# Low halves of the first weight pieces: from GpSimd beside the norm's products to VectorE behind them

## The chip, the cores and the metric
The kernel runs on one core of a Trainium2 chip. A core has TensorE (matrix products, into PSUM), VectorE, ScalarE and GpSimd (work on tiles of 128 rows), and SyncE, which issues transfers. Each engine runs its own instructions in order; semaphores make one wait for another. The profile calls them PE (PEld for its weight loads), DVE, ACT, POOL and SP. The metric is the device time of one execution in microseconds (us), lower is better.

## The reference
A trunk of two layers on x of 256 rows by 2048 columns, float32. Of each layer:

```python
for l in range(DEPTH):                     # 2
    h = rms_norm(x, norm_pre[l])
    proj = jnp.einsum('bsd,de->bse', h, w_in[l])
    (q, kc, vc, ksl, vsl, kwn, vwn, gl, z_att, u_s5, z_s5, u_pool, z_pool) = split(proj)
    att = nsa_mixer(...) * silu(z_att)     # three attention branches, gated
    ssm = s5_mixer(u_s5, ...) * silu(z_s5) # a diagonal state space layer
    pool = pool_mixer(u_pool, ...) * silu(z_pool)
    out = einsum(concatenate([att, ssm, pool]), w_out[l])
    x = x + rms_norm(out, norm_post[l])
```

`rms_norm` divides each row by the root of its mean square and multiplies by a weight per column. Every product with h waits for the norm, and the first norm of layer two waits for the end of layer one.

## The kernel before
Each float32 matrix product is made of three passes: both operands are split into a high part (a rounded copy, "fp32r") and a low part (what is left), and `mm3` (L384 to L389) adds high x high, high x low and low x high. The weights come as a stream of pieces of 2 x 128 x 1024 values per layer, in the order of use: the selected branch's values (`vs`, two pieces, four halves), the S5 input (`u5`, four pieces), keys and values, and so on to the output matrix (`wo`). SyncE loads a half into one of five `raw` buffers (L285); ScalarE makes the high part `whi` (L311); the low part `wlo` is raw minus high, on VectorE (L317) or, where the caller says so, on GpSimd (L315). The low part is the last to read the raw buffer, so it sets when the next load starts. The first three halves of `vs` have their high and low parts in tiles called `m`.

The rows are two tiles of 128. The norm of a tile: ScalarE sums the squares (L930), VectorE and GpSimd make the reciprocal norm (L395, L401, L402 and the power L396), VectorE multiplies x by it and by the weight in four products of 512 columns (`norm_scale`, L408), TensorE transposes the result (L415, through PSUM tiles `tr`, `sc`, `acc`, `sc`), ScalarE makes the high part of the transposed tile hT (L418) and VectorE its low part (L421). Then `vsel` multiplies a quarter of hT with a quarter of the `vs` weights: 12 matrix products (L387 to L389).

The two stages in question are written out by hand, and all five engines keep the written order there (`tc.manual_schedule(engines=ORDERED)`): the start, and the passage from layer one to layer two, where the last output products (`mm_last`), the update of x (L1230) and the next norm are interwoven. Between them a scheduler orders the instructions by its own estimate of the times.

At the start the lows of the four halves of `vs` go to GpSimd:

```python
r = rstd_of(sqs[0], first)
...
for h in range(2):
    split(0, h, True)(G)
...
r = rstd_of(sqs[1])
for h in range(2):
    split(1, h, True)(G)
```

In the passage the first half's low is VectorE's, the other three are GpSimd's. Where the program says `after("pool")`, what follows (S5's memsets L459, L460 and the load L1040) stands behind GpSimd's last instruction of the stage.

Of the kernel before, what the change touches and what calls it, by code (L numbers as in the profile page):

```python
# [17 lines left out]
S, D, NL = 256, 2048, 2  # L18
NKT = D // 128
SCALE = 128 ** -0.5  # L20
EPS = 1e-6
# [7 lines left out]

# column offsets of the input projection  # L30
OQ, OKC, OVC, OKS, OVS, OKW, OVW, OGL, OZA, OU5, OZ5, OUP, OZP = (
# [3 lines left out]
def piece_plan():  # L35
    """Weight pieces of one layer in the order of use: (kind, index, cols per half)."""
    b = [("vs", 0), ("vs", 1)] + [("u5", t) for t in range(4)]
    early = [("kc", 0), ("kc", 1), ("vc", 0), ("vc", 1), ("ks", 0), ("ks", 1), ("kw", 0), ("kw", 1),
             ("vw", 0), ("vw", 1), ("vw", 2)]
    cmp_ = [("ck", i) for i in range(4)] + [("cv", i) for i in range(4)]  # L40
    mid = []
    for i, e in enumerate(early):
        mid.append(e)
        if i >= 2:
            mid += cmp_[:2]
            del cmp_[:2]
    mid += cmp_
    pairs = []
    z5at = (1, 1, 1, 3)
    for p in range(4):  # L50
        pairs += [("q", 2 * p), ("za", 2 * p), ("q", 2 * p + 1), ("za", 2 * p + 1)]
        pairs += [("z5", t) for t in range(4) if z5at[t] == p]
    late = [("z5", t) for t in range(4) if z5at[t] > 3] + [("gl", 0), ("gl", 1)]
    for g in range(4):
        late += [("up", g), ("zp", g)]
    wo = [("wo", c * 4 + i) for c in range(4) for i in range(4)]
    return b + mid + pairs + late + wo
# [18 lines left out]

# columns of the per-layer small parameters
SM = {}
# [5 lines left out]
SMW = _o  # L84
# columns of the per-layer S5 matrices, pool and compression matrices
CBW = 1024
# [51 lines left out]
def body(ctx, tc, a):  # L138
# [39 lines left out]

# [1 line left out]
    cn = const.tile([128, CNW], F32, name="cn")  # L180
# [9 lines left out]

# [1 line left out]
    NP = NL * 16  # L192
# [12 lines left out]
    def after(key):  # L205
        """issue what follows behind the instruction kept under key, on its engine"""
        return tc.issue_after(X[key].ins)

    def s5_params():
# [41 lines left out]
        V.tensor_mul(ci, t2, t0)  # L251
        # cos and sin of 4 theta b and 32 theta a, a and b in 0 .. 7
        pa, pb = (st([128, NP, 16], "P", bufs=2) for _ in range(2))
# [14 lines left out]

# [1 line left out]
    stream = [(l, k, i, PIECE_OFF[n]) for l in range(NL) for n, (k, i) in enumerate(PLAN)]  # L270
# [51 lines left out]

# [1 line left out]
    chains = []  # L324
# [15 lines left out]
    def grab(*tags):  # L340
        """wait until every one of the tags has a free buffer, then hold them"""
        while not all(free(g) for g in tags):
            yield 0.0
        for g in tags:
            take(g)

    def demand(*tags):
        """the same for the stream of pieces: run the chains until the buffers are free"""
        while not all(free(g) for g in tags):
            forced[0] += 1  # L350
            slot(2.0)
        for g in tags:
            take(g)
# [21 lines left out]
    def split_f32r(hi, lo, src, scale=None, hi_eng=None):  # L375
        """hi + lo == src * scale, both float32r"""
        if scale is None:
            A.activation(hi, src, AF.Copy)  # L378
            V.tensor_tensor(lo, src, hi.bitcast(F32), op=ALU.subtract)
        else:  # L380
            A.activation(hi, src, AF.Copy, scale=scale)
            V.scalar_tensor_tensor(lo, src, scale, hi.bitcast(F32), op0=ALU.mult, op1=ALU.subtract)

    def mm3(out, l, r, start, stop, **kw):  # L384
        """three passes: hi*hi, hi*lo, lo*hi"""
        (lh, ll), (rh, rl) = l, r
        T.matmul(out, lhsT=lh, rhs=rh, start=start, stop=False, **kw)  # L387
        T.matmul(out, lhsT=lh, rhs=rl, start=False, stop=False, **kw)  # L388
        T.matmul(out, lhsT=ll, rhs=rh, start=False, stop=stop, **kw)  # L389

# [1 line left out]
    def rstd_of(parts_, first=None):  # L392
        """(sum of the four parts / D + EPS) ** -0.5; first: what rstd_first made of three of them"""
        s = first or rstd_first(parts_)
        V.scalar_tensor_tensor(s[:, 1:2], parts_[:, 3:4], 1.0 / D, s[:, 0:1], op0=ALU.mult, op1=ALU.add)  # L395
        X["pool"] = G.tensor_tensor(s[:, 2:3], s[:, 1:2], mhalf, op=ALU.pow)  # L396
        return s[:, 2:3]
# [7 lines left out]
    def norm_scale(x, r, gpre, hbuf, c):  # L405
        """hbuf = x * r * gpre in quarter c of x and hbuf [128, D]"""
        cs = slice(c * 512, (c + 1) * 512)
        V.scalar_tensor_tensor(hbuf[:, cs], x[:, cs], r, gpre[:, cs], op0=ALU.mult, op1=ALU.mult)  # L408

    def norm_high(t, hbuf, hT, c):  # L410
        """high part of quarter c of hbuf transposed; returns what makes the low part"""
        p = (trp, scp, accp, scp)[c]()
        for j in range(4):
            k = 4 * c + j
            T.transpose(p[:, j * 128:(j + 1) * 128], hbuf[:, k * 128:(k + 1) * 128], ident)  # L415
        sl = (slice(None), slice(4 * c, 4 * c + 4), slice(t * 128, (t + 1) * 128))
        pv = p.rearrange("p (k s) -> p k s", k=4)
        X["act"] = A.activation(hT[0][sl], pv, AF.Copy)  # L418

        def low():  # L420
            X["norm"] = V.tensor_tensor(hT[1][sl], pv, hT[0][sl].bitcast(F32), op=ALU.subtract)  # L421
        return low

    def vsel(n, t, c):
        """values of the selected branch, tile t, from quarter c of hT"""
        if t == 0 and c == 0:
# [4 lines left out]
    def norm_vsel(n, t, x, r, gpre, hbuf, hT, lag):  # L431
        """the norm of tile t and its values, quarter after quarter"""
        low = []
# [13 lines left out]

# [1 line left out]
    def s5_chain(l):  # L449
# [22 lines left out]
        def tables(hf):  # L472
            """cos and sin of 4 theta j, j = 8 a + b, for the state tiles 8 hf .. 8 hf + 7"""
            pa, pb = (z.rearrange("p (i a b) -> p i a b", i=8, a=8) for z in ms[:2])
# [28 lines left out]
        def spread(dst, x, y, op, k0):  # L503
            """x op y, group by group into the block diagonal of dst"""
            V.tensor_tensor(x, x, y, op=op)  # L505
# [42 lines left out]
        for t in range(4):  # L548
# [4 lines left out]
            kb = kbd  # L553
            # transposed input matrices and the lag kernels
            yield from grab("sc")
# [78 lines left out]

# [1 line left out]
    def cmp_blocks(which, g, p, l):  # L636
# [55 lines left out]

# [1 line left out]
    def rope(p, dst_hi, dst_lo):  # L694
# [7 lines left out]

# [1 line left out]
    def att_unit(pr, j, t):  # L704
        """one head of the pair, one tile of queries: scores .. transposed weights"""
        h = 2 * pr["p"] + j
# [4 lines left out]
        p = scp()  # L711
# [129 lines left out]

# [1 line left out]
    def pool_chain(g, l):  # L843
# [35 lines left out]
    def silu2(dst, p):  # L879
        """dst = 2*silu(p)"""  # L880
        A.activation(dst, p, AF.Tanh, scale=0.5)
        V.scalar_tensor_tensor(dst, dst, 1.0, p, op0=ALU.add, op1=ALU.mult)

# [1 line left out]
    def mm_b(n, h, p):  # L885
# [45 lines left out]

    # start
    xt = [a8([128, D]) for _ in range(2)]
# [14 lines left out]
    with tc.manual_schedule(engines=ORDERED):  # L948
# [33 lines left out]
        gp_out(1)  # L982
        for h in range(2):
            split(0, h, True)(G)
        def sq1(c):
# [6 lines left out]
        norm_scale(xt[0], r, gpre, hb[0], 2)  # L992
        norm_scale(xt[0], r, gpre, hb[0], 3)
        sq1(0)
        low = []
# [4 lines left out]
        for f in low:  # L1000
            f()
        r = rstd_of(sqs[1])
        for h in range(2):
            split(1, h, True)(G)
        for c in range(4):
            norm_scale(xt[1], r, gpre, hb[1], c)
        vsel(0, 0, 0)
        vsel(0, 0, 1)
# [15 lines left out]
    while n < nst:  # L1024
# [167 lines left out]
        else:  # L1192
# [32 lines left out]
            def update(t, r, sq=None):  # L1225
                """x += og * r, with the sums of squares or the store"""
                x, og = X["xt"][t], X["og"][t]
# [20 lines left out]
            elif q == 0:  # L1248
# [14 lines left out]
                else:  # L1263
                    m = n + 4
                    sqs = [st([128, 4], "sq", bufs=4) for _ in range(2)]
                    with tc.manual_schedule(engines=ORDERED):
# [12 lines left out]
                        r = rstd_of(sqs[0])  # L1279
                        split(m, 1, True)(G)  # L1280
                        for c_ in range(4):
                            norm_scale(X["xt"][0], r, X["gpre"], X["og"][0], c_)
                        mm_last(1, 2)
                        split(m + 1, 0, True)(G)
                        X["hT"] = hT
                        low = [norm_high(0, X["og"][0], hT, c_) for c_ in range(4)]
                        split(m + 1, 1, True)(G)
                        for f in low:
                            f()
                        mm_last(1, 3)  # L1290
                        first = rstd_first(X["osq"][1])
# [97 lines left out]
```

## Time and profile before

| | |
|---|---|
| time, median of 3 runs | 893.35 us (893.23 to 893.95) |
| span of the profiled execution (the page gives no other time for it) | 890.6 us |
| median less span | 2.75 us |
| TensorE busy | 857.6 us, 96% of the span |
| VectorE busy | 645.3 us, 72% |
| ScalarE busy | 481.3 us, 54% |
| GpSimd busy | 51.8 us, 6% |
| DMA | 165.75 MB, mean 186 GB/s |

A busy share is a mean over stages with different limits. What an engine waits for, and when, stands in the timelines; idle time of an engine that nobody waits for costs nothing.

### The profile page before, as it was taken

How to read it: one execution, taken by the hardware profiler on the slowest of the kernel's cores; microseconds unless marked ns; L12 is line 12 of the kernel's file. 1: busy time of each engine (PE TensorE's matmuls, PEld its weight loads, DVE VectorE, ACT ScalarE, POOL GpSimd, SP SyncE). 2: the span in 40 equal slices, each digit the busy share in tenths (PEclk: the TensorE clock that was granted, in tenths of full speed). 3: DMA queues.
4: the chain of work that ended last, by engine and by line, in shares of the span. 5: the costliest groups of instructions: out<-in, count | busy, mean ns of one | idle time of the engine just before them, and what ended most of it. 6: DMA issues, size and time to landing. Idle time of an engine off the chain costs nothing. (4 is left out here: it accounts for less than half of the span.)

```text
span 890.6 us, 17313 instructions
## 1 busy us (share of the span) xinstructions
PE 857.6 (96%) x6848; PEld 795.3 (89%) x6848; DVE 645.3 (72%) x1264; ACT 481.3 (54%) x933; POOL 51.8 (6%) x71
## 2 busy tenths in 40 slices
PE   4899999999999999999979999999999999999996
PEld 3898889999999999888869988999999999998884
DVE  6886779796987866556478556978968878665563
ACT  5454635676566754445445525475847767344440
POOL 3302000000000000000040300000000000000000
PEclk9899999999999999999989999999999999999998
DMA  7565766524344665456445558663534347455642
GB/s 288 179 188 185 268 235 225 172 104 162 121 165 143 227 241 194 172 201 224 182 165 199 183 197 312 211 213 99 173 123 155 140 144 295 154 177 189 197 146 95
DMA packets 46042, 165.75 MB, mean 186 GB/s; under 512 B 5508, under 2 KB 5764, under 8 KB 44808
## 3 DMA queue, kind: packets, MB, share of 16 engines
q1 hardware_dynamic: 43352, 154.15, 50.3%
q0 software_dynamic: 2608, 10.49, 3.3%
q8 instruction: 54, 0.88, 0.4%
q14 instruction: 28, 0.23, 0.1%
HBM read 159.37 MB, written 4.19 MB: 184 GB/s over the span
## 5 line engine op out<-in xcount | busy, mean ns | idle before, releaser
L311 ACT ACTIVATE whi<-raw 128x1024 fp32r<-128x1024 f32 (+2 forms) x238 | 248.4, 1046 | 256.3 <-PE pp L388 82.8
L317 DVE TENSOR_TENSOR wlo<-raw,whi 128x1024 fp32r<-128x1024 f32 (+1 forms) x236 | 284.4, 1207 | 123.7 <-ACT whi L311 123.1
L389 PE MATMUL pp<-hT,wlo 128*128 128x256 f32 x1280 | 365.7, 286 | 0.5 <-DVE wlo L317 0.5
L387 PE MATMUL pp<-hT,whi 128*128 128x256 f32 x1280 | 364.8, 285 | 0.8 <-ACT whi L311 0.8
L388 PE MATMUL pp<-hT,whi 128*128 128x256 f32 x1280 | 363.5, 284 | 0.0
L387 PEld LDWEIGHTS pp<-hT,whi 128*128 128x128 f32 x1280 | 245.0, 191 | 6.1 <-issue 3.8
L389 PEld LDWEIGHTS pp<-hT,wlo 128*128 128x128 f32 x1280 | 245.0, 191 | 2.4 <-DVE wlo L317 0.7
L388 PEld LDWEIGHTS pp<-hT,whi 128*128 128x128 f32 x1280 | 245.0, 191 | 1.7 <-issue 1.0
L387 PE MATMUL acc<-whi,m 128*128 128x512 f32 x112 | 44.4, 397 | 0.0
L389 PE MATMUL acc<-whi,m 128*128 128x512 f32 x112 | 44.4, 397 | 0.0
L388 PE MATMUL acc<-wlo,m 128*128 128x512 f32 x112 | 44.1, 394 | 0.0
L388 PE MATMUL pp<-wlo,m 128*128 128x512 f32 x112 | 43.6, 389 | 0.0
L389 PE MATMUL pp<-whi,m 128*128 128x512 f32 x112 | 43.6, 389 | 0.0
L387 PE MATMUL pp<-whi,m 128*128 128x512 f32 x112 | 43.6, 389 | 0.0
L507 ACT ACTIVATE m<-m 64x256 f32<-64x256 f32 x64 | 26.4, 413 | 5.9 <-DVE m L505 4.9
L728 ACT ACTIVATE P<-sc,sv 128x128 f32<-128x128 f32 (+1 forms) x64 | 26.2, 418 | 5.4 <-DVE sv L726 3.7
L925 POOL DMA_DIRECT2D a<-in_gpost x2 | 1.1, 557 | 451.4 <-PE tr L743 451.4
L378 ACT ACTIVATE a<-tr 128x256 fp32r<-128x256 f32 (+1 forms) x32 | 15.6, 488 | 18.6 <-PE tr L743 18.5
L387 PEld LDWEIGHTS acc<-whi,m 128*128 128x128 f32 x112 | 21.5, 192 | 4.5
L388 PEld LDWEIGHTS acc<-wlo,m 128*128 128x128 f32 x112 | 21.5, 192 | 4.5
L389 PEld LDWEIGHTS acc<-whi,m 128*128 128x128 f32 x112 | 21.4, 191 | 4.5
L736 ACT ACTIVATE P<-P,sv 128x128 f32<-128x128 f32 (+1 forms) x64 | 25.4, 448 | 0.0
(295 smaller groups left out, 1384.4 us busy)
## 6 DMA issues: line engine op xcount, KB each, us to landing
raw<-in_w SPq DMA_DIRECT2D x272, 512.0 KB, 3.6
raw<-in_w SPq DMA_DIRECT2D x8, 420.0 KB, 4.2
a<-in_x SPq DMA_DIRECT2D x4, 512.0 KB, 6.9
a<-in_gpost POOLq DMA_DIRECT2D x2, 1024.0 KB, 4.8
a<-in_x POOLq DMA_DIRECT2D x2, 1024.0 KB, 6.3
xs<-a SPq DMA_DIRECT2D x2, 1024.0 KB, 4.1
a<-xs POOLq DMA_DIRECT2D x2, 1024.0 KB, 7.4
out_dram<-a SPq DMA_DIRECT2D x8, 256.0 KB, 2.4
```

Source lines behind the costliest of these rows:

```text
L311: A.activation(hi[:, :w], raw[:, :w], AF.Copy)
L317: V.tensor_tensor(lo[:, :w], raw[:, :w], hi[:, :w].bitcast(F32), op=ALU.subtract)
L378: A.activation(hi, src, AF.Copy)
L387: T.matmul(out, lhsT=lh, rhs=rh, start=start, stop=False, **kw)
L388: T.matmul(out, lhsT=lh, rhs=rl, start=False, stop=False, **kw)
L389: T.matmul(out, lhsT=ll, rhs=rh, start=False, stop=stop, **kw)
L507: A.activation(dst[64 * g:64 * g + 64, :, k0:k0 + 4, 16 * g:16 * g + 16], x[64 * g:64 * g + 64], AF.Copy)
L728: A.activation(P[:, b], pv[:, b], AF.Exp, scale=SCALE, bias=sv[:, 1, b:b + 1], accum_out=sv[:, 2, b:b + 1])
L736: A.activation(P[:, b], P[:, b], AF.Copy, scale=sv[:, 4, b:b + 1])
L925: nc.gpsimd.dma_start(g, bass.AP(tensor=src.tensor, offset=src.offset, ap=[[0, 128], [1, D]]))
```

## The change
At the start, the lows of the first `vs` piece are made on VectorE, one behind the products of tile 0 and one behind the hT lows of tile 0; those of the second piece behind the products of tile 1. In the passage, the three lows that were GpSimd's are made on VectorE behind the hT lows of tile 0, and ScalarE's highs for them stand behind its own part of the transposed tile. GpSimd keeps the powers L396, its loads and its memsets. Lines behind the first hunk move by one or two numbers. (Comments were taken out as well; those lines are left out here.)

```diff
         r = rstd_of(sqs[0], first)
         gp_out(1)
-        for h in range(2):
-            split(0, h, True)(G)
+        wlow = [split(0, h, True) for h in range(2)]
+
         def sq1(c):
...
         norm_scale(xt[0], r, gpre, hb[0], 2)
         norm_scale(xt[0], r, gpre, hb[0], 3)
+        wlow[0](V)
         sq1(0)
         low = []
         for c in range(4):
...
         for f in low:
             f()
+        wlow[1](V)
         r = rstd_of(sqs[1])
-        for h in range(2):
-            split(1, h, True)(G)
         for c in range(4):
             norm_scale(xt[1], r, gpre, hb[1], c)
+        for h in range(2):
+            split(1, h)
         vsel(0, 0, 0)
         vsel(0, 0, 1)
...
                         r = rstd_of(sqs[0])
-                        split(m, 1, True)(G)
                         for c_ in range(4):
                             norm_scale(X["xt"][0], r, X["gpre"], X["og"][0], c_)
                         mm_last(1, 2)
-                        split(m + 1, 0, True)(G)
                         X["hT"] = hT
                         low = [norm_high(0, X["og"][0], hT, c_) for c_ in range(4)]
-                        split(m + 1, 1, True)(G)
                         for f in low:
                             f()
+                        split(m, 1)
+                        split(m + 1, 0)
+                        split(m + 1, 1)
                         mm_last(1, 3)
```

VectorE's order at the start before, from the last products of tile 0 (L408 into `a_7_88`) to the first hT low of tile 1 (`hT_85` from `tr_237`):

```order
L408 SCALAR_TENSOR_TENSOR a_7_88<-a_1_82,rs_139,a_11_92 128x512 x2
L421 TENSOR_TENSOR hT_85<-tr_160,hT_84 128x4x128
...
L421 TENSOR_TENSOR hT_85<-sc_182,hT_84 128x4x128
L401 TENSOR_REDUCE rs_194<-sq_87 128x1
...
L408 SCALAR_TENSOR_TENSOR a_8_89<-a_2_83,rs_194,a_11_92 128x512 x4
L421 TENSOR_TENSOR hT_85<-tr_237,hT_84 128x4x128
```

The same place now; `m_26`, `m_27`, `m_37` and `wlo_207` are the lows of the four `vs` halves, `raw_...` their raw buffers:

```order
L408 SCALAR_TENSOR_TENSOR a_7_88<-a_1_82,rs_139,a_11_92 128x512 x2
L317 TENSOR_TENSOR m_26_146<-raw_102,m_26_146 128x1024
L421 TENSOR_TENSOR hT_85<-tr_159,hT_84 128x4x128
...
L421 TENSOR_TENSOR hT_85<-sc_181,hT_84 128x4x128
L317 TENSOR_TENSOR m_27_148<-raw_104,m_27_148 128x1024
L401 TENSOR_REDUCE rs_194<-sq_87 128x1
...
L408 SCALAR_TENSOR_TENSOR a_8_89<-a_2_83,rs_194,a_11_92 128x512 x4
L317 TENSOR_TENSOR m_37_203<-raw_108,m_37_203 128x1024
L317 TENSOR_TENSOR wlo_207<-raw_110,whi_206 128x1024
L421 TENSOR_TENSOR hT_85<-tr_237,hT_84 128x4x128
```

Four L317 have come into this queue; the hT lows are the same as before, with other buffer numbers.

GpSimd's order at the start, before, from the first power to the load of the pool matrices:

```order
L396 TENSOR_TENSOR rs_139<-rs_139,mhalf 128x1
L315 TENSOR_TENSOR m_26_146<-raw_102,m_26_146 128x1024
L315 TENSOR_TENSOR m_27_149<-raw_104,m_27_149 128x1024
L396 TENSOR_TENSOR rs_194<-rs_194,mhalf 128x1
L315 TENSOR_TENSOR m_37_199<-raw_108,m_37_199 128x1024
L315 TENSOR_TENSOR wlo_203<-raw_110,whi_202 128x1024
L1040 DMA pw_430<-in_pw 128x1024
```

Now the four L315 are gone, and the load and the memsets follow the second power directly.

VectorE's order in the passage, from the products of tile 0 of layer two to the last output product of tile 1 (L1222, now L1224):

```order
 L408 SCALAR_TENSOR_TENSOR a_637_4611<-a_643_4619,rs_5213,a_640_4615 128x512 x4
...
+L421 TENSOR_TENSOR hT_5194<-sc_5252,hT_5193 128x4x128
+L317 TENSOR_TENSOR m_759_5262<-raw_5081,m_759_5262 128x1024
+L317 TENSOR_TENSOR m_760_5265<-raw_5087,m_760_5265 128x1024
+L317 TENSOR_TENSOR wlo_5269<-raw_5089,whi_5268 128x1024
 L401 TENSOR_REDUCE rs_5284<-sq_4618 128x1
 L402 TENSOR_SCALAR rs_5284<-rs_5284 128x1
-L1222 TENSOR_TENSOR a_638_4612<-acc_5078,a_639_4613 128x512
+L1224 TENSOR_TENSOR a_638_4612<-acc_5078,a_639_4613 128x512
```

Three L317 now stand between the last hT low of tile 0 and the reciprocal norm of tile 1.

## Rows read from the trace of the kernel before

**Rows 1.** Busy us by stretch: PE, PEld, DVE, ACT, POOL (instructions), granted clock, DMA share, GB/s.

```profile
0.00:40.00 40.00, 24.34 (x140) 22.00 (x141) 29.54 (x53) 19.18 (x37) 15.76 (x17) 0.91 0.68 243
40.00:440.00 400.00, 399.35 (x3256) 371.17 (x3255) 295.55 (x602) 224.13 (x435) 11.46 (x21) 1.00 0.54 189
440.00:475.00 35.00, 28.28 (x168) 25.11 (x167) 26.95 (x41) 18.33 (x36) 13.07 (x12) 0.85 0.44 153
...
25.00:30.00 5.00, 2.96 (x14) 2.99 (x15) 4.84 (x6) 1.87 (x4) 2.98 (x3) 0.57 0.76 261
...
430.00:435.00 5.00, 5.00 (x23) 4.13 (x22) 0.00 (x0) 0.00 (x0) 0.00 (x0) 1.00 0.26 98
...
465.00:470.00 5.00, 4.96 (x28) 4.52 (x29) 3.88 (x7) 1.79 (x3) 0.73 (x2) 0.66 0.45 144
```

**Rows 2.** Timeline of VectorE, first stage: start, us, instruction, count [idle before].

```profile
10.21 3.51 DVE L408 SCALAR_TENSOR_TENSOR a<-a,rs,a 128x512 f32<-128x512 f32 x2
13.65 0.68 DVE L973 COPY a<-pp 128x512 f32<-128x512 f32 x1
...
14.85 2.30 DVE L408 SCALAR_TENSOR_TENSOR a<-a,rs,a 128x512 f32<-128x512 f32 x2
...
20.02 0.14 DVE L401 TENSOR_REDUCE rs<-sq 128x1 f32<-128x3 f32 x1
...
21.29 6.93 DVE L408 SCALAR_TENSOR_TENSOR a<-a,rs,a 128x512 f32<-128x512 f32 x4 [0.67 <-POOL rs L396]
28.14 0.68 DVE L421 TENSOR_TENSOR hT<-tr,hT 128x512 fp32r<-128x512 f32 x1
...
31.57 3.50 DVE L317 TENSOR_TENSOR wlo<-raw,whi 128x1024 fp32r<-128x1024 f32 x3 [0.22 <-ACT whi L311]
```

**Rows 3.** Timeline of GpSimd, first stage.

```profile
10.72 5.21 POOL L315 TENSOR_TENSOR m<-raw,m 128x1024 fp32r<-128x1024 f32 x2 [0.54 <-ACT m L311]
...
23.55 2.80 POOL L315 TENSOR_TENSOR wlo<-raw,whi 128x1024 fp32r<-128x1024 f32 x1
...
27.01 0.97 POOL L459 MEMSET m<- 128x1024 f32 x1
```

**Rows 4.** View of line L408: ns minimum/median/maximum, and who waited for it.

```profile
L408 DVE SCALAR_TENSOR_TENSOR a<-a,rs,a x16: 739/750/2847, 10.2 to 466.9; 128x512 f32<-128x512 f32 x16
...
PE sc L415: 5.9, 3
```

**Rows 5.** Timeline of TensorE, first stage.

```profile
27.04 1.09 PE L415 MATMUL sc<-cn,a 128*128 128x128 f32 x4 [2.13 <-DVE a L408]
...
29.48 0.56 PE L387 MATMUL pp<-m,hT 128*128 128x256 f32 x1
...
32.73 0.28 PE L387 MATMUL pp<-m,hT 128*128 128x256 f32 x1
32.84 0.28 PE L388 MATMUL pp<-m,hT 128*128 128x256 f32 x1
...
39.56 0.28 PE L387 MATMUL pp<-hT,whi 128*128 128x256 f32 x1
```

**Rows 6.** Timeline of VectorE, passage to layer two.

```profile
444.55 6.93 DVE L408 SCALAR_TENSOR_TENSOR a<-a,rs,a 128x512 f32<-128x512 f32 x4 [0.66 <-POOL rs L396]
...
454.36 0.15 DVE L402 TENSOR_SCALAR rs<-rs 128x1 f32<-128x1 f32 x1
457.10 0.69 DVE L1222 TENSOR_TENSOR a<-acc,a 128x512 f32<-128x512 f32 x1 [2.59 <-PE acc L389]
...
464.11 2.08 DVE L408 SCALAR_TENSOR_TENSOR a<-a,rs,a 128x512 f32<-128x512 f32 x3 [0.66 <-POOL rs L396]
```

**Rows 7.** Timeline of TensorE, passage to layer two.

```profile
462.53 0.28 PE L389 MATMUL pp<-whi,hT 128*128 128x256 f32 x1
465.01 0.63 PE L415 MATMUL tr<-cn,a 128*128 128x128 f32 x4 [2.20 <-DVE a L408]
```

**Rows 8.** Busy us of the stretch behind the first norm, columns as in Rows 1.

```profile
31.15:75.63 44.48, 44.48 (x367) 44.48 (x367) 38.70 (x102) 23.21 (x40) 10.71 (x20) 0.98 0.61 190
```

## The prediction
> **What bounds the kernel now.** I read the busy table by stage first [rows 1]. TensorE works 399.35 of the 400 us between 40 and 440, and about as densely in the second layer; it stands still for 15.7 us in the first 40 and for 6.7 us between 440 and 475. So only these two stages, the norms at the head of each layer, can give time back, and all else follows TensorE. The second view was VectorE's timeline in the first stage [rows 2]: its L408 rows are the norm's products (x times reciprocal norm times weight, 512 columns), and they take 3.51 us for two, 2.30 for two and 6.93 for four. The third was GpSimd's timeline beside it [rows 3]: while L315 (a low half) runs, one product gets through, and it ends when L315 ends. The line's own view [rows 4] gives the free price, median 750 ns against a maximum of 2847, and names TensorE's transposes as what waits for them. Then came TensorE around the first stage [rows 5], and VectorE and TensorE around the second [rows 6, 7].
>
> The profiled execution has a span of 890.6 us; the median of the runs is 893.35, so 2.75 lie around the span, and I carry a gain in the span over to the median unchanged.
>
> **The change part by part.** It takes seven L315 off GpSimd (two of them fill 5.21 us) and puts seven L317 of the same shape on VectorE. Three L317 in a row take 3.50, the last of them 1.22 [rows 2], so one costs a queue (3.50 − 1.22) / 2 = 1.14 us. ScalarE's and TensorE's products stay the same in number. No wait on GpSimd is left for a weight low.
>
> *First layer, VectorE's queue.* A free product costs a queue 0.67 (in layer two, with no L315 beside them, three take 2.08 [rows 6], of which the last is 0.74, the line's minimum [rows 4]). From the first product at 10.21 to the first hT low of tile 1 there stand eight products, 8 x 0.67 = 5.36; two copies, 14.85 − 13.65 = 1.20; the four new lows, 4 x 1.14 = 4.56; four hT lows of a copy's shape, 4 x 0.60 = 2.40; and the reciprocal norm, 21.29 − 20.02 = 1.27 [rows 2]. Sum 14.79, so that hT low starts at 25.0, where it stands at 28.14 now: 12.5 of products became 5.36, the lows cost 4.56, and 0.6 of short waits has gone.
>
> *First layer, TensorE.* Its 24 products of the first two weight quarters need the second new low (done near 18.8) and end by 21. The four groups of transposes follow tile 1's products, which now run from 20.0 to 22.8, so they end at 23.5 to 23.9. The third quarter needs the third new low, two places before 25.0: 25.0 − 2 x 1.14 + 1.22 = 23.94. It starts there, and at 29.48 now [rows 5]: 5.5 us. From it to the first product of the next piece stand 72 products, at 0.12 apiece (32.73 to 32.84, rounded) 8.64 us; now they take 39.56 − 29.48 = 10.08, because the first of them ran at half pace after TensorE had waited for the products. The wait for the first hT low (done 25.7, when fourteen products are through) costs about 0.1. So the next piece starts near 32.6 and not 39.56: 7.0 us.
>
> *What is late next there.* TensorE comes 7.0 us earlier to the pieces that follow, VectorE only 31.15 − 27.4 = 3.7 (its four hT lows of tile 1 end the norm). VectorE is busy 38.70 of the 44.48 us that follow, while TensorE never rests [rows 8], so of its 5.8 us of slack it has to win back 3.3 before the S5 tables are used, near 76. Most of that slack is waiting for TensorE to free weight buffers, which now happens earlier. I charge 0.4.
>
> The loads: the first two raw buffers come free near 15.3 and 18.8 instead of at the ends of L315 (near 13.2 and 15.9), so the two pieces that reuse them are issued two to three microseconds later on SP; they are wanted by ScalarE only behind the norm, near 26, and by TensorE after 32. GpSimd's load of the pool matrices and its memset, queued behind L315 until 26.3, come at about 20, beside tile 1's products. The memset of 0.97 us at 27.01 [rows 3] already ran beside two products that took the free 0.67 a step, so I cost it at nothing; held for all of it, one product would add 0.97.
>
> *Second layer.* VectorE's queue from 444.55: four products 2.68, four hT lows 2.40, three new lows 3.42, the two small ones of the reciprocal norm 0.38, so L1222 of tile 1 can start at 453.4, and now starts at 457.10 [rows 6]. TensorE does not hold it: the last product ends at 447.3, its transposes by 448.4, and the twelve output products behind them, at 5.00 / 22 = 0.23 each (23 begin in 5 us [rows 1]), end by 451.2. Three raw buffers are given back by the new lows, two of them some us later than by L315, far ahead of the pieces they are loaded for. ScalarE makes the three highs after the transposed tiles, from 448.7, a microsecond before VectorE comes to the first low, so the lows need not wait. Everything from L1222 to tile 1's transposes is a chain through ScalarE and GpSimd that the change doesn't touch, so it moves by 3.65 us, and the transposes from 465.01 to 461.35.
>
> TensorE, though, finishes its 48 products of tile 0 near 456.9 (451.2 + 48 x 0.12) and then stands some 4.5 us, where it now stands 2.20 [rows 7]. Behind 2.20 us of rest the granted clock reads 0.66 in the next 5 us, that is the lower level of 1.2 GHz for part of it [rows 1]. The Trainium skill ("TensorE: Matmul & The Clock Gate", What's actually happening) says that throttled is the default state and activity releases it, so a longer rest speaks against this part of the change; no run so far shows a rest of 4.5 us here. If the clock behaved as it does now, the stage would win 3.65; if the transposes run at the lower level from the start (1.09 for four at 27.04 against 0.63 at 465.01 [rows 5, 7]), it wins 3.65 less some 0.6. I take the latter, 3.05.
>
> Sum: 7.0 − 0.4 + 3.05 = 9.65 us; the span 881.0, the time 893.35 − 9.65 = 883.7.
>
> **Rivals.**
> *VectorE becomes the bound in layer one.* For it: 38.70 of 44.48 busy [rows 8], and 4.56 us more on its queue. Against: its slack. If it wins nothing back, TensorE keeps VectorE's 3.7 instead of 7.0 and no charge: 3.7 + 3.05, time 886.6.
>
> *TensorE's clock falls in both stages.* For it: the granted clock was 0.57 between 25 and 30 [rows 1], behind a wait of 2.13 [rows 5]. Against: the new waits in stage one are well under a microsecond. If it falls as now, layer one loses the 1.44 of the products (10.08 − 8.64) and three times 0.46 on transposes (1.09 − 0.63 [rows 5, 7]), layer two another 1.2, twice the charge it has: 4.0 back, 887.7.
>
> *The products are slow of themselves (slower).* They might be slowed by the transfers into the same memory, since DMA was busy beside the first four, and not by L315. Then they keep their time, and the lows come on top: 4.56 in layer one; in layer two, 454.36 + 0.2 + 3.42 = 458.0 against 457.10, 0.9. Time 898.8. The point from which it decides: the eight products of layer one cost the queue 12.5 us now (3.44 + 2.21 + 6.85), 1.56 each, so above 1.56 − 4.56 / 8 = 0.99 us apiece the edit loses. Against it: the last four of layer two, without L315 beside them, are at 0.67 [rows 6]. The Trainium skill ("SBUF — State Buffer", Who interferes with whom) describes an exclusive lock between GpSimd's reads and a VectorE operation with two inputs in SBUF, held for a whole instruction; by that the products fall to 0.67 and this rival is void, and the rows, where product and L315 end together, agree.
>
> *Hidden anyway (no change).* If the weight stream set the pace between the norms, an earlier start would be given back in waits for loads. Against: 399.35 of 400 busy, DMA at 0.54 [rows 1]. Time then about 893.
>
> **How the numbers follow.** Forecast 0.60 (its own range 882.0 to 885.5: stage one within a microsecond, the clock of stage two between nothing and 1.3); VectorE's bound 0.20; the clock 0.12; slower 0.04; no change 0.04. The range runs from 881.5 (882.7 with neither charge, and 1.2 for short waits of TensorE that I can't place) to 888.5, which takes in both smaller gains. A measurement tells 0.2%, 1.8 us, from no change: faster 0.92, same 0.04, slower 0.04.
>
> **What would show it.** L408 at 0.75 throughout and no L315; the third quarter's first product near 24 and the next piece near 32.6; no TensorE wait between 33 and 80 longer than half a microsecond; L1222 of tile 1 nine microseconds after the first product of tile 0, directly behind the three lows; a rest of TensorE near 4.5 us before tile 1's transposes. It is wrong if products stay above 1 us, if the TensorE waits move into the S5 part, or if the stage behind the second norm grows by more than the 0.6.

## The result, and the profile after

The kernel after takes 881.58 us (median of 4 runs, 880.47 to 882.04), the kernel before 893.29 beside it: ratio 0.9878, 95% interval 0.9865 to 0.9891. Forecast were 883.7 in a range of 881.5 to 888.5, so the time is 2.1 us below the forecast and at the lower end of the range. The span of the profiled execution went from 890.6 to 880.1 us.

Busy time of the kernel after, first line of its page, then the stretches of [rows 1] (PE, PEld, DVE, ACT, POOL with instructions, granted clock, DMA share, GB/s):

```profile
PE 851.2 (97%) x6848; PEld 790.0 (90%) x6848; DVE 640.5 (73%) x1271; ACT 481.2 (55%) x933; POOL 33.5 (4%) x64
```

```profile
0.00:40.00 40.00, 28.18 (x194) 25.14 (x195) 30.76 (x70) 25.36 (x49) 5.45 (x13) 1.00 0.77 266
40.00:440.00 400.00, 397.73 (x3230) 369.19 (x3229) 296.14 (x599) 221.61 (x432) 12.02 (x22) 1.00 0.57 190
440.00:475.00 35.00, 30.25 (x230) 29.18 (x229) 30.59 (x48) 20.39 (x37) 4.58 (x8) 0.95 0.60 204
25.00:30.00 5.00, 5.00 (x43) 4.99 (x43) 5.00 (x10) 2.79 (x4) 2.00 (x4) 1.00 0.71 213
```

GpSimd fell from 15.76 to 5.45 us in the first 40. VectorE rose by only 1.2 there, though it has four lows of 1.2 more: its eight products of the start fell from 12.7 us (3.51, 2.30, 6.93) to 5.6 (1.42, 1.41, 2.74), and other work came forward into the stretch (70 instructions for 53). TensorE works 28.18 of the first 40 where it worked 24.34 [rows 1], and the stretch from 25 to 30, granted 0.57 before, is full at 1.00. The middle holds a first surprise: TensorE stands still for 2.3 us between 40 and 440 where it stood for 0.65.

The line of the norm's products, which answers to [rows 4], then VectorE in the first stage, which answers to [rows 2]:

```profile
L408 DVE SCALAR_TENSOR_TENSOR a<-a,rs,a x16: 743/746/754, 10.7 to 457.2; 128x512 f32<-128x512 f32 x16
```

```profile
10.66 1.42 DVE L408 SCALAR_TENSOR_TENSOR a<-a,rs,a 128x512 f32<-128x512 f32 x2
...
14.51 1.22 DVE L317 TENSOR_TENSOR m<-raw,m 128x1024 fp32r<-128x1024 f32 x1
...
18.04 1.21 DVE L317 TENSOR_TENSOR m<-raw,m 128x1024 fp32r<-128x1024 f32 x1
...
20.45 2.74 DVE L408 SCALAR_TENSOR_TENSOR a<-a,rs,a 128x512 f32<-128x512 f32 x4 [0.67 <-POOL rs L396]
23.11 1.22 DVE L317 TENSOR_TENSOR m<-raw,m 128x1024 fp32r<-128x1024 f32 x1
24.24 1.22 DVE L317 TENSOR_TENSOR wlo<-raw,whi 128x1024 fp32r<-128x1024 f32 x1
25.38 0.68 DVE L421 TENSOR_TENSOR hT<-tr,hT 128x512 fp32r<-128x512 f32 x1
```

All sixteen products now take 743 to 754 ns; the maximum was 2847. The four of tile 1 take 2.74 us where they took 6.93, the four new lows stand where the order put them, and the first hT low of tile 1 comes at 25.38.

TensorE in the first stage and at the next piece, which answers to [rows 5]:

```profile
19.31 0.39 PE L388 MATMUL pp<-m,hT 128*128 128x256 f32 x1 [0.86 <-DVE m L317]
...
21.35 0.63 PE L415 MATMUL tr<-cn,a 128*128 128x128 f32 x4 [0.46 <-DVE a L408]
...
23.72 0.36 PE L387 MATMUL pp<-m,hT 128*128 128x256 f32 x1
24.38 0.39 PE L388 MATMUL pp<-m,hT 128*128 128x256 f32 x1 [0.29 <-DVE m L317]
...
33.29 0.28 PE L389 MATMUL pp<-hT,wlo 128*128 128x256 f32 x1
```

The third quarter starts at 23.72 (before 29.48), the next piece at 33.29 with two of its products done earlier (before 39.56). Of the waits on VectorE behind tile 0's transposes 0.86, 0.46 and 0.29 are left; the 0.86 is for the second new low, which is done at 18.04 + 1.21 = 19.25.

The passage, VectorE and then TensorE, which answer to [rows 6] and [rows 7]:

```profile
438.27 2.74 DVE L408 SCALAR_TENSOR_TENSOR a<-a,rs,a 128x512 f32<-128x512 f32 x4 [0.66 <-POOL rs L396]
...
443.33 2.36 DVE L317 TENSOR_TENSOR m<-raw,m 128x1024 fp32r<-128x1024 f32 x2
445.61 1.22 DVE L317 TENSOR_TENSOR wlo<-raw,whi 128x1024 fp32r<-128x1024 f32 x1
446.75 0.15 DVE L401 TENSOR_REDUCE rs<-sq 128x1 f32<-128x3 f32 x1
...
447.00 0.68 DVE L1224 TENSOR_TENSOR a<-acc,a 128x512 f32<-128x512 f32 x1
...
453.99 2.08 DVE L408 SCALAR_TENSOR_TENSOR a<-a,rs,a 128x512 f32<-128x512 f32 x3 [0.66 <-POOL rs L396]
```

```profile
454.88 1.08 PE L415 MATMUL tr<-cn,a 128*128 128x128 f32 x4 [4.66 <-DVE a L408]
455.76 1.06 PE L415 MATMUL sc<-cn,a 128*128 128x128 f32 x4
456.62 1.06 PE L415 MATMUL acc<-cn,a 128*128 128x128 f32 x4
457.33 0.56 PE L387 MATMUL pp<-m,hT 128*128 128x256 f32 x1
457.69 0.35 PE L388 MATMUL pp<-m,hT 128*128 128x256 f32 x1
```

L1224 (L1222 before) of tile 1 stands 8.73 us behind the first product of tile 0, where it stood 12.55, directly behind the lows and the small ones. TensorE then rests 4.66 us and comes back at the lower level (1.08 for four transposes); products are short again from 457.69.

To see where the time comes from, I compared the starts of the same ScalarE instructions in two traces. Gain against the kernel before, medians over stretches of before's time:

```
stretch (us)        25-75     150-425   460-500   from 575
after               6.3-6.5   6.28      10.59     10.54
after, second run   6.0-6.2   7.60      11.98     13.13
```

The start gives 6 us by its end and the passage 4.3 to 4.4 in both runs; layer two behind it gives nothing back, and the second run wins 1.2 more there. Between 75 and 150 the two executions of one program differ by 1.3 us, and by 1.2 in layer two: that is how far one profile can be trusted.

### The profile page after: what moved, and what is told of

Its sections match the earlier page's. It is cut to its first block, busy times and chain, and to the rows that moved or that the text cites. A ratio compares the mean times of both kernels' runs of the same rounds, so it can differ in the third digit from the quotient of the medians.

```text
span 880.1 us, 17310 instructions
## 1 busy us (share of the span) xinstructions
PE 851.2 (97%) x6848; PEld 790.0 (90%) x6848; DVE 640.5 (73%) x1271; ACT 481.2 (55%) x933; POOL 33.5 (4%) x64
## 5 line engine op out<-in xcount | busy, mean ns | idle before, releaser
L317 DVE TENSOR_TENSOR wlo<-raw,whi 128x1024 fp32r<-128x1024 f32 (+2 forms) x238 | 286.7, 1207 | 125.7 <-ACT whi L311 125.0
L389 PEld LDWEIGHTS pp<-whi,m 128*128 128x128 f32 x112 | 21.0, 188 | 4.4
```

The costliest lines, as they stand in the source:

```text
L317: V.tensor_tensor(lo[:, :w], raw[:, :w], hi[:, :w].bitcast(F32), op=ALU.subtract)
```

## The experiments

Three comparisons, each with the kernel before beside the others: it measured 891.33, 891.42 and 891.37 us, some 2 us less than beside the first runs of the kernel after, so the ratios to it are what compares. The recorded ratio is not the plain quotient of the two medians; it lies up to 0.0014, or 1.2 us, beside it, and so a gain is good to about a microsecond. The kernel after, run again in the third, measured 880.99 us, 0.9882 (0.9865 to 0.9899).

### The start alone, the passage alone

```diff
 # e1_start: the kernel after, but in the passage as before
                         r = rstd_of(sqs[0])
+                        split(m, 1, True)(G)
...
+                        split(m + 1, 0, True)(G)
...
+                        split(m + 1, 1, True)(G)
-                        split(m, 1)
-                        split(m + 1, 0)
-                        split(m + 1, 1)
 # e2_passage: the kernel before with the opposite edit there
```

> The start of the kernel after, the passage into layer two of the kernel before (its three low halves on GpSimd again). Theory A (the products of the norm take about four times as long while GpSimd makes a low half, at both places and independently): the start's gain alone, read as 6.3 us at L1224 of the first tile, so 893.3 - 6.3 = 887.0 us; the products L408 of the passage stay at 6.93 us for four. Rival B (the two places are worth the same thing only together, since TensorE takes up in one what the other gives): under 884 or over 890.

> The start of the kernel before, the passage of the kernel after. Theory A: the passage's gain alone, read as 4.3 us at the first product of the pair u5 in layer two, so 893.3 - 4.3 = 889.0 us, with the products of the passage at 2.74 us for four and those of the start as before (3.5 and 2.3 us for two). With this and the run of the start alone the two gains should add to the whole of 11.7 us within 1 us. Rival B: they do not add.

Start alone: 882.83 us, ratio 0.9896 (0.9881 to 0.9911), 8.5 us below before. Passage alone: 888.89 us, 0.9965 (0.9951 to 0.9979), 2.4 us. Together 10.9, and the kernel after gained 10.4 in the third comparison: they add within a microsecond, so theory A holds on that. By the ratios they are 9.3 and 3.1, together 12.4 against 10.5, so they add only within two. 882.83 is below the 884 that I had named as rival B's sign; that 884 stood for a gain of 9.3 from 893.3, and the gain here is 8.5 from 891.33, so it does not speak for B. The sizes missed: the start is worth 2.2 more than the 6.3 I had read from one profile, the passage 1.9 less than 4.3. In the start-alone kernel the passage is untouched; VectorE's products there, then TensorE's transposes of tile 1:

```profile
434.96 6.93 DVE L408 SCALAR_TENSOR_TENSOR a<-a,rs,a 128x512 f32<-128x512 f32 x4 [0.67 <-POOL rs L396]
```

```profile
455.08 0.63 PE L415 MATMUL tr<-cn,a 128*128 128x128 f32 x4 [2.21 <-DVE a L408]
455.75 1.09 PE L415 MATMUL sc<-cn,a 128*128 128x128 f32 x4
456.63 1.06 PE L415 MATMUL acc<-cn,a 128*128 128x128 f32 x4
```

The same 6.93 as before, with the start's products at 1.42, 1.41 and 2.74: the slowness belongs to the place where GpSimd's lows are, not to the kernel.

### Is it GpSimd's being busy, its reading, or its two inputs?

```diff
 # e3_memset
-                X["pool"] = G.tensor_tensor(lo[:, :w], raw[:, :w], hi[:, :w].bitcast(F32), op=ALU.subtract)
+                for _ in range(3):
+                    X["pool"] = G.memset(lo[:, :w].bitcast(F32), 0.0)
 # e4_copy
+                X["pool"] = G.tensor_copy(lo[:, :w], raw[:, :w])
```

> The kernel before with each low half of its seven early ones replaced by three fills of the same buffer with zero on GpSimd, at the same place: GpSimd is as busy beside the products but reads nothing. Seven low halves of weights are left out by that. Theory A (what holds VectorE's product is GpSimd's operation with two tensors read, not that GpSimd works): products of the norm at 0.74 us each, no low half in VectorE's queue: 876 to 880 us. Rival E (any work of GpSimd holds a VectorE product): products at 0.97 us or more, 884 us or more.

> The kernel before with GpSimd copying the raw half into the low one (one tensor read) where it subtracted (two tensors read); the seven low halves are then not the ones wanted. Theory A in its narrow form (only two tensors read on GpSimd hold a product with two tensors read on VectorE): products at 0.74 us each, 876 to 880 us. In its wide form (any reading operation of GpSimd holds it): products as long as the copy beside them, 879 to 888 us.

With fills: 876.53 us, 0.9833 (0.9812 to 0.9853). With copies: 883.91 us, 0.9911 (0.9893 to 0.9928). GpSimd and VectorE beside each other, first with the fills (lines are one number higher there):

```profile
19.07 2.97 POOL L316 MEMSET m<- 128x1024 f32 x3
21.98 2.98 POOL L316 MEMSET wlo<- 128x1024 f32 x3
```

```profile
19.15 2.74 DVE L409 SCALAR_TENSOR_TENSOR a<-a,rs,a 128x512 f32<-128x512 f32 x4 [0.67 <-POOL rs L397]
```

and with the copies:

```profile
20.48 1.04 POOL L315 CAST m<-raw 128x1024 fp32r<-128x1024 f32 x1
21.46 1.50 POOL L315 CAST wlo<-raw 128x1024 fp32r<-128x1024 f32 x1
```

```profile
20.57 4.27 DVE L408 SCALAR_TENSOR_TENSOR a<-a,rs,a 128x512 f32<-128x512 f32 x4 [0.67 <-POOL rs L396]
```

Beside 2.97 us of fills the four products take their free 2.74; beside copies that read one tensor, 4.27, two of the four being held to 1.50 and 1.52. So what holds a product is GpSimd reading, with one input as well as with two: the wide form of theory A. Rival E, that any work of GpSimd holds it, is out. The Trainium skill ("SBUF — State Buffer", Who interferes with whom) says the same: a VectorE instruction with two SBUF inputs contends with a GpSimd instruction that reads SBUF, not with one that only writes it. Both runs agree with it. The copy on VectorE at 13.65 in [rows 2], which reads only a PSUM tile, took 0.68 beside a running L315 [rows 3]; that an operation with a single SBUF input goes free as well is not shown here.

The fills leave no low on either engine's way, so the kernel after at 880.99 against 876.53 also says what the seven lows cost on VectorE: 4.5 us of their 8.0 (7 x 1.14). The traces place it in both stages: 2.0 us by 76 us, and 2.6 in the passage, of which some 0.8 is the lower level of TensorE's clock behind the longer rest, which the kernel with fills does not have.

### The lows in front of the products, and the lows twice

```diff
 # e5_front: the kernel before, at all five places
-            split(0, h, True)(G)
+            split(0, h, True)(V)
 # e6_twice: the kernel after, all seven
+                    V.tensor_tensor(lo[:, :w], raw[:, :w], hi[:, :w].bitcast(F32), op=ALU.subtract)
```

> The kernel before with the seven low halves on VectorE but at the places where GpSimd had them: in front of the norm's products, not behind them. Theory A (the engine is what counts, the place only shifts VectorE's own queue): products at 0.7 us each; at the start the two lows of the first split (2.4 us) now stand in front of the first tile's products and two more in front of the second's, in the passage nothing else than their length in front of the four products: 881.6 plus 2.5 to 5 = 884 to 887 us. Rival C (the place behind the products is what counts): about 893, no better than before. Rival D (VectorE has room for them anywhere): 881.6.

> The kernel after with each of the seven new low halves made twice on VectorE, which changes no result. Theory A (VectorE's queue is the path in both places, so that a low half there costs its length): two lows of 1.15 us in the first stage ahead of the next transposes or products that TensorE waits for, about 4.4 us, and three, 3.4 us, in the passage: about 889 us. Rival D (behind the products VectorE has slack): under 883.5.

In front: 885.57 us, 0.9921 (0.9904 to 0.9938), so by the medians the engine gives 5.8 of the 10.4 us and what is left the other 4.6. Its six runs lie between 882.75 and 887.01, and by the ratios it is 7.0 of 10.5, so the split is rough. By the starts of ScalarE's instructions, as above, the place behind the products is worth 1.9 us by 76 us (4.4 against 6.3) and 1.6 in the passage (2.7 against 4.3), 3.5 in all; about 1 of the 4.6 belongs to an order of TensorE's products that the two kernels do not share (see the charge of 0.4 below). Twice: 890.7 us, 0.9989 (0.9978 to 1.0), 9.7 above the kernel after (in another comparison), more than the 8.0 that the second lows last. Theory A is right in both and too low for the second. VectorE with the second lows (L319 there), and TensorE's transposes of tile 1 at the start and in the passage (L417 there):

```profile
26.37 1.22 DVE L317 TENSOR_TENSOR m<-raw,m 128x1024 fp32r<-128x1024 f32 x1
27.62 1.22 DVE L319 TENSOR_TENSOR m<-raw,m 128x1024 fp32r<-128x1024 f32 x1
28.77 1.22 DVE L317 TENSOR_TENSOR wlo<-raw,whi 128x1024 fp32r<-128x1024 f32 x1
```

```profile
25.09 1.05 PE L417 MATMUL tr<-cn,a 128*128 128x128 f32 x4
...
466.14 1.09 PE L417 MATMUL tr<-cn,a 128*128 128x128 f32 x4 [6.43 <-DVE a L410]
```

Both come at the lower level, the second behind a rest of 6.43 us where the kernel after has 4.66. So VectorE's queue is on the path in both stages: of the first seven lows 3.5 us were hidden, of seven more nothing, and the lower level came on top.

### TensorE's rest, and VectorE's order

```diff
 # e7_reorder: the kernel after, start
-        wlow[1](V)
         r = rstd_of(sqs[1])
+        wlow[1](V)
 # and passage
                         split(m, 1)
-                        split(m + 1, 0)
-                        split(m + 1, 1)
+                        later = [split(m + 1, h_, True) for h_ in range(2)]
...
                         ev_wo(1, 3)
+                        later[0](V)
                         r = rstd_of(X["osq"][1], first)
+                        later[1](V)
 # e8_fill: the kernel after, behind the four vsel(m, 0, c_)
+                        pf = scp()
+                        for k_ in range(36):
+                            T.matmul(pf[:, :256], lhsT=hT[0][:, 0, :128], rhs=X["mix", 3][:, 0, 0, :256], start=True, stop=True)
 # e9_both28: both, with 28 products; e10_pass: the same without the edit at the start
```

> The kernel after with VectorE's queue in another order: at the start the second low half of the first split goes behind the second tile's reciprocal root (so that ScalarE and the products begin one low half earlier), in the passage only one low half stands ahead of the evictions and the reciprocal root, the two others go behind these. Theory A (VectorE's queue is the path there): 0.6 us at the start and up to 1.5 us in the passage, about 879.5 us. Rival F (TensorE, 97% busy, gives it back): 881.6 us.

> The kernel after with 36 extra products of TensorE, whose result nothing uses, in its rest of the passage (behind the eviction products of vsel(m,0), ahead of the transposes of the second tile). Theory G (the rest is what lowers the granted clock behind it): granted 1.00 from the transposes on, these at 0.63 us where they took 1.08, the time 0.5 to 1.2 us lower: about 880.8 us. Rival H (the low stretch is hidden behind VectorE's evictions and products): 881.6. If the extra products last longer than the rest, it is slower by what they overrun.

> The kernel after with both edits: VectorE's queue in the other order at start and passage, and 28 extra products (whose result nothing uses) in TensorE's rest of the passage. Theory A with G (both gains are TensorE's and add, the rest being only 3.5 us in the reordered kernel): 0.9 us from the reordering and 0.9 to 2.1 us from the extra products below the kernel after, 877.5 to 878.7 us where after is 880.5. Rival F: the order at the start costs 0.7 us, since there TensorE's clock rose later; then no better than the extra products alone, 878.3 us.

> The kernel after with VectorE's queue reordered in the passage alone (its start as in the kernel after) and 28 extra products in TensorE's rest there. Theory A with G: 0.6 us from the order and 0.9 us from the extra products by the traces, about 879.0 us where after is 880.5; lower than the version with both orders if the order at the start costs time. Rival H: nothing, 880.5 us.

> The kernel after once more, unchanged, beside the other versions on one chip: 0.9878 of the kernel before, near 880.5 us where before measures 891.4. Two things are read from its profile: whether the 2.1 us that TensorE waited for weight halves between 60 and 430 us in the first profile of after come again (Theory S: they belong to the kernel, the transfers arriving earlier against the same use; Rival: they come and go between executions, as the 0.5 us of the run with extra products suggests), and the length from L1224 of the first tile to the last transposes of the passage, 28.3 us in the first profile.

Reordered: 879.65 us, 0.9864 (0.9845 to 0.9883). Extra products: 878.34 us, 0.9853 (0.9834 to 0.9872). Both: 878.21 us, 0.9846 (0.9829 to 0.9863). Passage order and extra products: 876.27 us, 0.9827 (0.9812 to 0.9841), 4.7 below the kernel after in the same comparison, and the fastest of all.

For the passage theories A and G hold. By the starts of ScalarE's instructions it gives 4.3 and 4.4 us in the two runs of the kernel after, 4.9 reordered, 5.2 with the extra products and 6.3 with both. So of the 4.7 the edits give 2.0; another 1.2 lie ahead of the passage, where the two kernels are the same program (8.84 at 150 us against 7.60). I had expected 879.0; of the difference to 876.27 the traces place only a part.

For the start the order costs 1.9 us by the medians (878.21 against 876.27), as rival F has it, but its cause is not shown. In the reordered kernel TensorE had the higher level only from 23.4 us, and the third quarter came 13.96 behind the first product, where the kernel after has 13.06; this is the clock of which rival F speaks. In the kernel with both, which has the same start, the higher level was there at 16 us and the third quarter came 12.84 behind, sooner than in the kernel after. Its gain at 150 us is 7.14 where passage order and extra products have 8.84; of these 1.7 us 0.84 lie ahead of the first product (11.36 and 10.52) and 1.1 behind 76 us, in a part that is the same in both, while 0.2 was won between.

TensorE with the extra products, behind which the transposes of tile 1 stand:

```profile
448.46 4.48 PE L1303 MATMUL sc<-m,hT 128*128 128x256 f32 x36
453.19 0.66 PE L415 MATMUL tr<-cn,a 128*128 128x128 f32 x4 [0.25 <-DVE a L408]
453.94 0.63 PE L415 MATMUL sc<-cn,a 128*128 128x128 f32 x4
454.51 0.66 PE L415 MATMUL acc<-cn,a 128*128 128x128 f32 x4
```

They run at 0.63 to 0.66 where they took 1.06 to 1.09, and from tile 1's first product to its last transposes pass 456.54 − 452.38 = 4.16 us against 457.67 − 452.69 = 4.98 in the second run of the kernel after: 0.8 us, as theory G has it. Of the median's 2.65 (878.34 against 880.99, in different comparisons) that is the part which the trace shows.

In the second run of the kernel after, what it was repeated for:

```profile
PE pp L389 <- DVE wlo L317: 0.7, 2, 0.4
```

TensorE's waits for weight halves between 34 and 430 us are 0.7, where the first profile of the same program has

```profile
PE pp L387 <- ACT whi L311: 1.3, 2, 1.0
PE pp L389 <- DVE wlo L317: 0.8, 1, 0.8
```

so theory S fell: these waits come and go between executions (0.5 in before, none in the start-alone kernel). The length from L1224 of the first tile to the last transposes was 28.24 us, 28.30 in the first profile.

## Why the prediction was right, and where its sizes were off

- *The cause.* Right: products at a free 0.67 a step and no longer, at both places. The rival that they are slow of themselves or by the transfers fell with the first profile: between 10.2 and 14.0 us the DMA share was 0.99 before, with a product of 2.84, and 1.02 after, with every product at 0.75. The fills and copies then showed what the prediction had only taken from rows: it is GpSimd's reading. One reading of the rows was off: a held product does not end when L315 ends but 0.55 us behind it, in all six cases before (first 13.72 behind 13.18).
- *VectorE's queue at the start.* Forecast 25.0 for the first hT low from a first product at 10.21; it was 25.38 from 10.66, that is 24.93 on the forecast's clock.
- *TensorE at the start.* Third quarter 23.94 forecast, 23.72 measured, and 6.2 us earlier by the distance from the first product (13.06 in four executions, 19.27 before) where 5.5 was forecast: its first product needs only a high, and the low is needed 0.66 later. The next piece came at 33.29 less two products, 6.5 us earlier, 7.0 when the later first product is taken out. Forecast 7.0.
- *The charge of 0.4 for the part behind.* This is the step that failed. I charged a loss; from the next piece to 150 us the executions gained between nothing (the first profile) and 2.2 us (start alone); gain and waits for weight halves add to 1.9 to 2.4 in the five that share this start (the two of the kernel after, start alone, extra products, passage order). From the next piece's third product to the first tile's L1222 the same products took 397.2 us before and 395.1 in the start-alone kernel. Part of it is before's own 0.65 of rest. The rest goes with something that the prediction left out: behind the start, in the S5 part (77 to 133 us in before), the scheduler put TensorE's products in another order in every kernel that makes these lows on VectorE behind the products. The products of the compressed keys and values begin 5.4 us behind the first S5 transposes (L563, at 76.5) in before and 3.2 behind them (at 70.7) in the kernel after:

```profile
L1111 PE MATMUL acc<-raw,a x128: 379/379/404, 81.9 to 118.9; 128*32 128x256 f32 x128
```

```profile
L1113 PE MATMUL acc<-raw,a x128: 379/379/403, 73.9 to 111.3; 128*32 128x256 f32 x128
```

  From the next piece to 76 us each kernel's gain stands still (6.51 in the first profile, 7.41 in the start-alone kernel); it changes in this part and stands still again up to the passage. The fills, the lows in front and the passage alone keep before's order, and there gain and waits add to 0.6 to 0.9. So 1 to 1.8 us goes with the other order; no run changed the order alone, so that it is the cause is not shown. VectorE did not become the bound: TensorE's longest wait for it there was 0.8. One sign that I had set for being wrong, TensorE's waits in the S5 part, did come in the first profile (2.1 us between 100 and 125), but not as a fixed cost: 0.7 in the second run, none in the start-alone kernel.
- *The passage.* L1222 forecast 3.65 earlier, measured 3.82. Of the whole passage I forecast 3.05; by ScalarE's starts it gave 4.3 and 4.4 in the kernel after and 3.65 in the passage-alone kernel, so this term was too small as well, by 0.6 to 1.3. The charge of 0.6 for the clock had the wrong sign in the first profile: from tile 1's first product to its last transposes pass 5.07 us after (4.98 in the second run) and 5.54 before. The transposes did come at the lower level from the start, as forecast, but TensorE had the higher one back 2.8 us after it resumed; before, it kept the higher for the first 1.3 us and then fell, until 469.35. In the passage-alone kernel the same distance is 5.73, 0.2 longer. So the charge measures −0.6 to +0.2. Its whole size was 1.3: the runs with no low stretch need 4.16 to 4.24.
- *The sum.* Forecast 6.6 for the start and 3.05 for the passage; the two halves alone gave 8.5 and 2.4 by the medians. The total of 9.65 stands against 11.7 in the first comparison and 10.4 in the later one. The error of 2.1 us is the start's charge and the passage's, less the waits for weight halves, and the spread between executions and comparisons.
- *Around the span.* I carried 2.75 us; the run of the kernel after that was profiled shows 881.88 − 880.1 = 1.78, and its other runs the same. 2.75 was the median of other executions against one execution's span, so it held the spread between executions and not a fixed cost.

## What to carry to other kernels

When an operation's duration varies by four with the same shape, look for an instruction of another engine behind whose end it always ends by the same time (here 0.55 us); here that named the cause before any run. Work that GpSimd reads for is not free beside VectorE operations with two SBUF inputs; beside copies from PSUM it cost them nothing here. Moving it costs VectorE's queue, so put it behind what TensorE waits for (roughly 6 us from the engine, 3.5 from the place). A new start can make a scheduler order the part behind it in another way: compare the order of the products before pricing that part. A rest of TensorE that cannot be removed may be filled with products nobody needs, if the clock is down behind it; with the last two lows behind the eviction, that gave 2.0 us more in the passage.

## What the runs showed that was not expected

- The same rest does not always cost the same. Behind 2.20 us of rest the transposes of the passage fell to 1.09 in before and in the start-alone kernel, and in the copy kernel they did not:

```profile
454.45 0.63 PE L415 MATMUL tr<-cn,a 128*128 128x128 f32 x4 [2.20 <-DVE a L408]
455.11 0.63 PE L415 MATMUL sc<-cn,a 128*128 128x128 f32 x4
455.77 0.63 PE L415 MATMUL acc<-cn,a 128*128 128x128 f32 x4
```

- At the start TensorE's products took a 0.21 step up to 22.14 us in before, to 17.4 in the kernel after, and already 0.12 from 15.7 in the start-alone kernel; with the other order at the start to 23 us in one kernel and to 16 in another. When the higher level comes is not fixed by the program alone, and with that order it is worth a microsecond (third quarter 13.96 and 12.84 behind the first product).
- The norm's products of two executions of one program agree to 0.01 us; the difference of 2.6 us between their spans lies in TensorE's waits for weights, 2.1 against 0.7 us in layer one and 1.2 against none in layer two.
- GpSimd is held too: L315 took 2.38 us alone (at 454.56) and 2.80 where a VectorE product was still under way at its start (at 23.55).
